# Attention on one core: six of the eight value products of the later queries split, masks side by side, and row maxima and the splits of w_o moved to earlier steps

## The chip, the cores and the metric

The kernel runs as one program on one core of a Trainium2 chip. The metric is the device time of one execution in microseconds (us); the time before is the median of three runs. A core has five engines that work side by side, each through its own queue in order: TensorE (PE in the profile, with its weight loads shown apart as PEld), VectorE (DVE), ScalarE (ACT), GpSimd (POOL) and SyncE (SP, which here only issues DMAs). PE reads SBUF and writes PSUM; DVE and ACT read and write both.

## The reference

Two layers of a decoder over 1024 positions. The change is in the attention of the first layer: 12 heads of dense causal attention (query and key of 96 columns, value of 64), in float32.

```python
def one_block(args):
    q_blk, n = args
    t_idx = n * Q_BLOCK + jnp.arange(Q_BLOCK)
    sc = jnp.einsum('bqhd,bkhd->bhqk', q_blk, k,
                    preferred_element_type=jnp.float32) * scale
    mask = k_idx[None, :] <= t_idx[:, None]
    sc = jnp.where(mask[None, None], sc, NEG)
    p = jax.nn.softmax(sc, axis=-1).astype(v.dtype)
    return jnp.einsum('bhqk,bkhd->bqhd', p, v)
```

Its result, with that of four more heads over a memory, goes through one output projection, `x = x + concat(mix, cross) @ w_o[i]`, and then through an MLP. The second layer has another attention, which the change does not touch.

## The kernel before

**Split products.** For most products of float32 accuracy a value is split in two parts, `hi` (rounded to the type float32r) and `lo` (the rest): `split` (lines 97 to 103) makes `hi` on ACT (line 99) and `lo` on DVE (line 100). A product is then three products of float32r: hi by hi, hi by lo, lo by hi. The alternative is one "whole" product in float32, which the profile shows as two records.

**One head.** For head h, `head_tiles` brings the 96 rows of query and key by four DMAs on SP's queue and splits them into qh, ql, kh, kl; there are three sets of these tiles, so it runs for head h + 2 while head h is computed. `row_max(h, i)` computes the scores of the 128 queries of tile i once, on PE, into the PSUM tile psx (two banks wide, one buffer, for tiles 4 to 7; a one-bank tile for 0 to 3), adds a causal mask with one bfloat16 product (identb by dmask, line 730), and lets DVE take the negative maximum of each row (line 731). After all eight tiles, `max_row` turns the maxima round on PE (psxt), splits them (mh, ml) and writes them by two DMAs on SP's queue as the 97th row of qh and ql, so that every later score has its row's maximum subtracted.

**Steps.** The scores are then computed again, transposed, in blocks: G is the half of the queries (0 earlier, 1 later, 512 columns each) and k the block of 128 keys. A block on the diagonal has fewer columns: for G = 1 the blocks 0 to 4 have 512, the blocks 5, 6 and 7 have 384, 256 and 128; for G = 0 the blocks 0 to 3 have 512, 384, 256 and 128. That makes NB = 12 blocks, or steps, a head, in the order of the table `blocks` (the last head has its own, `blocks_end`). Step n in program order is:

- `scores` (line 852): three products into a tile pss, with a mask product (identb by dmaskT) for a block on the diagonal; then ACT takes the exponential p (line 862), and p is split into ph and pl unless the block is "whole";
- the row maxima of a later head that the dictionary `ahead` assigns to step n;
- `values` (line 882) of the block of three steps ago (LV): for a whole block p by vf, for a split one ph by vh and ph by vl; and of the block of five steps ago (LB) the late third product, pl by vh. They add up in the tile pso, one for each G.

In steps with a narrow (128 column) block the score and value products are issued alternately. `v_tiles` (step 6 of a head) makes vh, vl and vf of the next head, with vf a full copy; a column of ones beside v gives the softmax's denominators. The finished pso goes through ACT (`on`, line 910) and two DMAs on SP; the denominators of heads 0 to 5, 6 to 9 and 10 are inverted in one go each (`rc_split`: DVE, ACT, and two DMAs rTq and rTk) and multiplied in by `rc_mul` (products psrc, lines 951 and 952, and a DVE multiplication). The last head is divided at once (`last_o`).

**What sets the order.** The recording layer keeps each engine's order close to that of the program, but may move a product behind a later one that does not wait for it. All DMAs of the stage are on SP's queue.

**w_o.** The first half of w_o is loaded and split during the last heads by `wq.step()`: eight actions (`load` or `split`, lines 628 and 99/100, tiles wor and woq, 128 by 1024 elements each), one every second step from step 120 (`n >= 10 * NB and n % 2 == 0`). The output projection (pswo, lines 108 to 110) follows the attention directly.

## Time and profile before

| | us |
|---|---|
| median of 3 runs | 2187.11 |
| lowest and highest of them | 2183.63, 2187.38 |
| the profiled execution, its own time | 2188.19 |
| its span, first to last instruction | 2186.5 |
| first score product of the attention stage starts (pss, line 852) | 253.40 |
| first product of w_o starts (pswo, line 108) | 488.30 |
| first product of the MLP's first layer starts (psu) | 584.55 |

The attention stage lies in the fifth to ninth of the 40 slices of the page's second part. How to read the profile: PE's records overlap, since a product begins before the one ahead of it has left the array, and their ends are modelled; the distance from start to start is what one costs. "x2" is the number of records that a row merges. Text in square brackets is the time that the engine was idle before the row and what ended it. In a view of stretches each row gives the limits, the length, and then for PE, PEld, DVE, ACT and POOL the busy time and the number of instructions, the clock of PE that was granted (1.00 is full), and the busy share of the DMA engines.

### The profile page before, as it was taken

The numbers are of one execution on the slowest core, as the hardware profiler recorded it, in microseconds if no ns is written. First come the engines' busy times: TensorE is split into PE (matmuls) and PEld (weight loads), VectorE is DVE, ScalarE is ACT, GpSimd is POOL, SyncE is SP. The second block draws the span as 40 slices with busy tenths as digits, with TensorE's granted clock in tenths as the row PEclk, the third lists the DMA queues.
The fourth block names the chain that finished last, engine by engine and source line by source line (L and its number), as shares of the span: only waits on it lengthen the run. The fifth ranks groups of instructions, "written<-read, shape, count | busy, mean of one in ns | idle before, by whom it ended". The sixth has DMA issues, their size and how long they took to land.

```text
span 2186.5 us, 28912 instructions
## 1 busy us (share of the span) xinstructions
PE 2139.8 (98%) x9993; PEld 1714.4 (78%) x9993; DVE 1480.1 (68%) x2813; ACT 1009.6 (46%) x2142; POOL 162.1 (7%) x227
## 2 busy tenths in 40 slices
PE   6999999999999999999999899999999999999998
PEld 5888776668788888888888778668788888888886
DVE  7556667755987776786657443665987776885665
ACT  5455466654633333444445453774633333444452
POOL 0012100001000000000001133440000000000000
PEclk9999999989999999999999999999999999999999
DMA  7202222323254445964533111123254445954442
GB/s 248 64 3 62 53 62 48 94 82 117 78 178 149 143 140 175 342 195 126 165 116 97 63 39 49 39 78 103 80 175 148 159 156 177 323 186 145 126 120 87
DMA packets 171232, 272.97 MB, mean 125 GB/s; under 512 B 15713, under 2 KB 71758, under 8 KB 171086
## 3 DMA queue, kind: packets, MB, share of 16 engines
q1 hardware_dynamic: 164228, 253.80, 36.6%
q0 software_dynamic: 4016, 13.12, 1.6%
q10 hardware_dynamic: 2842, 4.22, 0.5%
q8 instruction: 78, 1.28, 0.2%
q14 instruction: 68, 0.56, 0.1%
HBM read 181.69 MB, written 76.81 MB: 118 GB/s over the span
## 4 chain that ended last, share of the span: by engine, by line
PE 87%; DVE 6%; ACT 2%; DMA 2%; issue 1%; POOL 0%; SPq 0%; DVEq 0%; ACTq 0%; POOLq 0%
PE psy L1601 5%; PE psy L1603 5%; PE psy L1602 5%; PE psu L1316 5%; PE psu L1317 5%; PE psu L1315 5%; PE psz L1601 4%; PE psz L1602 4%; PE psz L1603 4%; PE pss L852 4%; PE psv L1317 4%; PE psv L1316 4%; PE psv L1315 4%; PE pso L882 4%; PE pswo L110 2%; PE pswo L108 2%
## 5 line engine op out<-in xcount | busy, mean ns | idle before, releaser
L99 ACT ACTIVATE i<-mr 128x512 fp32r<-128x512 f32 x78 | 49.3, 632 | 122.3 <-PE psu L1316 42.9
L862 ACT ACTIVATE p<-pss 128x512 f32<-128x512 f32 (+2 forms) x144 | 68.4, 486 | 80.3 <-PE pss L852 76.8
L1601 PE MATMUL psy<-g 128*128 128x512 f32 x256 | 99.9, 390 | 0.0
L1602 PE MATMUL psy<-g 128*128 128x512 f32 x256 | 99.6, 389 | 0.0
L1603 PE MATMUL psy<-g 128*128 128x512 f32 x256 | 99.4, 390 | 0.0
L99 ACT ACTIVATE g<-i 128x512 fp32r<-128x512 f32 x79 | 49.7, 629 | 92.0 <-PE psz L1602 45.1
L100 DVE TENSOR_TENSOR g<-i,g 128x512 fp32r<-128x512 f32 x79 | 55.2, 699 | 48.8 <-ACT g L99 48.8
L731 DVE TENSOR_REDUCE m<-psx 128x1 f32<-128x768 f32 (+7 forms) x96 | 71.3, 752 | 24.9 <-PE psx L730 24.4
L99 ACT ACTIVATE uh<-i 128x512 fp32r<-128x512 f32 x66 | 41.6, 631 | 85.3 <-PE psy L1602 40.7
L100 DVE TENSOR_TENSOR uh<-i,uh 128x512 fp32r<-128x512 f32 x66 | 45.5, 689 | 45.0 <-ACT uh L99 44.9
L1601 PE MATMUL psz<-g 128*128 128x512 f32 x192 | 74.7, 389 | 0.0
L1603 PE MATMUL psz<-g 128*128 128x512 f32 x192 | 74.7, 389 | 0.0
L1602 PE MATMUL psz<-g 128*128 128x512 f32 x192 | 74.7, 389 | 0.0
L100 DVE TENSOR_TENSOR i<-mr,i 128x512 fp32r<-128x512 f32 x78 | 53.6, 687 | 24.5 <-ACT i L99 24.5
L852 PE MATMUL pss<-qh,kh 97*128 97x512 f32 (+2 forms) x144 | 65.9, 464 | 0.5 <-DMA qh<-mhl 0.5
L882 PE MATMUL pso<-p,vf 128*128 128x512 f32 (+3 forms) x152 | 64.9, 509 | 0.0
L99 ACT ACTIVATE i<-d 128x512 fp32r<-128x512 f32 x44 | 27.8, 633 | 70.6 <-PE psu L1316 39.6
L852 PE MATMUL pss<-ql,kh 97*128 97x512 f32 (+2 forms) x144 | 58.4, 406 | 0.0
L1526 DVE TENSOR_TENSOR mqf<-mqq,mqf 128x512 f32<-128x512 f32 x64 | 43.0, 685 | 20.4 <-DMA mqq<-in_mlp_w_down_dram 20.1
L1603 PEld LDWEIGHTS psy<-g 128*128 128x128 f32 x256 | 48.0, 188 | 10.0
L1601 PEld LDWEIGHTS psy<-g 128*128 128x128 f32 x256 | 48.1, 188 | 9.9
L1602 PEld LDWEIGHTS psy<-g 128*128 128x128 f32 x256 | 48.1, 188 | 9.8
(623 smaller groups left out, 6901.6 us busy)
## 6 DMA issues: line engine op xcount, KB each, us to landing
i<-hd SPq DMA_DIRECT2D x154, 256.0 KB
hd<-uh SPq DMA_DIRECT2D x76, 256.0 KB
hd<-ul SPq DMA_DIRECT2D x76, 256.0 KB
mr<-in_mlp_w_up_dram SPq DMA_DIRECT2D x36, 512.0 KB
hd<-x SPq DMA_DIRECT2D x72, 256.0 KB
mr<-hd SPq DMA_DIRECT2D x70, 256.0 KB
d<-in_mlp_w_up_dram SPq DMA_DIRECT2D x32, 512.0 KB
mqq<-in_mlp_w_down_dram SPq DMA_DIRECT2D x32, 512.0 KB
```

Of the source, the lines that this page charges most:

```text
L99: nc.scalar.activation(hi, src, AF.Copy)
L100: nc.vector.tensor_tensor(lo, src, f32(hi), ALU.subtract)
L731: nc.vector.reduce_max(m8s[h][:, i : i + 1], ps[:, :n], axis=AX, negate=True)
L852: return lambda: nc.tensor.matmul(o, a, b, skip_group_check=True, **kw)
L862: nc.scalar.activation(p[:, c0:], ps, AF.Exp, scale=SC)
L882: mms.append(lambda: nc.tensor.matmul(o, a, b, skip_group_check=True, **kw))
L1315: nc.tensor.matmul(ps, wh[:, k, :], xh[:, k, :], start=p in (1, 2, 5) and k == 0, stop=False, skip_group_check=True)
L1316: nc.tensor.matmul(ps, wh[:, k, :], xl[:, k, :], start=False, stop=False, skip_group_check=True)
L1317: nc.tensor.matmul(ps, wl[:, k, :], xh[:, k, :], start=False, stop=k == 3, skip_group_check=True)
L1601: nc.tensor.matmul(ps, ah[:, j, :], bh, start=p in (1, 5, 2) and k == 0, stop=False, skip_group_check=True)
L1602: nc.tensor.matmul(ps, ah[:, j, :], bl, start=False, stop=False, skip_group_check=True)
L1603: nc.tensor.matmul(ps, al[:, j, :], bh, start=False, stop=k == NP - 1, skip_group_check=True)
```

## The change

- **Products.** For G = 1 only the blocks 0 and 2 stay whole; 4, 5, 6 and 7 are now split as 1 and 3 were. In the last head the four blocks of G = 0, whole before, are split too. There is one more buffer each for ph and pl.
- **vf** has one buffer for all heads instead of two; its copy is made two steps after vh and vl (`v_full`, step 8), and its ones are set once.
- **Order of blocks.** The two tables are new.
- **Masks of one step side by side.** In a step that is not interleaved and has a block on the diagonal, the row maximum's products are recorded between the first score product and the mask, so that the two masks follow one another. DVE's reduction is recorded after the split of the step.
- **Earlier steps.** The row maxima (`ahead`) stand one step sooner, but for the first pair, `head_tiles` two steps sooner (step 0), and the actions on w_o begin at step 116 instead of 120, one in three steps.

```diff
@@ row_max
-        nc.vector.reduce_max(m8s[h][:, i : i + 1], ps[:, :n], axis=AX, negate=True)
+        return lambda: nc.vector.reduce_max(m8s[h][:, i : i + 1], ps[:, :n], axis=AX, negate=True)
@@ v_tiles
-        vb = (at.tile([P, NT, 128], F32R, name=f"vh{i}"), at.tile([P, NT, 64], F32R, name=f"vl{i}"), at.tile([P, NT, 128], F32, name=f"vf{i}"))
+        vb = (at.tile([P, NT, 128], F32R, name=f"vh{i}"), at.tile([P, NT, 64], F32R, name=f"vl{i}"))
         vbufs.append(vb)
+    vf = at.tile([P, NT, 128], F32, name="vf")
+    nc.gpsimd.memset(vf[:, :, 64:128], 1.0)
...
-        nc.vector.tensor_copy(vf[:, :, 0:64], src)
-    blocks = [(1, 0), (0, 0), (1, 4), (0, 1), (1, 5), (0, 2), (1, 6), (0, 3), (1, 7), (1, 1), (1, 2), (1, 3)]
-    blocks_end = [(1, k) for k in (0, 1, 4, 3, 5, 2, 6, 7)] + [(0, k) for k in range(4)]
+    blocks = [(1, 0), (0, 0), (1, 4), (0, 1), (1, 2), (0, 2), (1, 5), (0, 3), (1, 1), (1, 6), (1, 7), (1, 3)]
+    WHOLE = {(1, 0), (1, 2)}
+    blocks_end = [(1, k) for k in (0, 4, 2, 5, 1, 6, 7, 3)] + [(0, k) for k in range(4)]
-    def whole(h, G, k):
-        return k not in (1, 3) if G else h == H - 1
@@ scores, then()
-            if whole(h, G, k):
-                probs[(h, G, k)] = (p,)
+            if (G, k) in WHOLE:
+                probs[(h, G, k)] = p
                 return
-            ph = at.tile([P, 512], F32R, tag="ph", bufs=3, name=f"ph{h}_{G}_{k}")
-            pl = at.tile([P, 512], F32R, tag="pl", bufs=4, name=f"pl{h}_{G}_{k}")
+            ph = at.tile([P, 512], F32R, tag="ph", bufs=4, name=f"ph{h}_{G}_{k}")
+            pl = at.tile([P, 512], F32R, tag="pl", bufs=5, name=f"pl{h}_{G}_{k}")
@@ values
+        if (G, k) in WHOLE:
+            if late:
+                return [], lambda: None
+            mm(po[:, c0:], vf[:, k, :], probs.pop((h, G, k))[:, c0:], start=first, stop=last)
+        elif late:
             mm(po[:, c0:], vh[:, k, :], probs.pop((h, G, k, "late"))[:, c0:], start=False, stop=last)
         else:
+            ph, probs[(h, G, k, "late")] = probs.pop((h, G, k))
+            mm(po[:, c0:], vh[:, k, :], ph[:, c0:], start=first, stop=False)
+            mm(po[0:64, c0:], vl[:, k, :], ph[:, c0:], start=False, stop=False)
+            last = False
@@ the loop over steps
+    def v_full(h):
+        nc.vector.tensor_copy(vf[:, :, 0:64], v[:, :, h * 64 : (h + 1) * 64])
...
-        for i, d in ((7, -4), (6, -2), (5, 0), (3, 1), (4, 2), (2, 3), (1, 5), (0, 6), (8, 7)) if h > 1 else ...
+        for i, d in ((7, -5), (6, -3), (5, -1), (4, 1), (3, 2), (2, 3), (1, 4), (0, 5), (8, 6)) if h > 1 else ...
...
-        for f in mix + ms:
+        rows_ = []
+        if mix or len(ms) < 4:
+            for f in mix + ms:
+                f()
+            ms = []
+        else:
+            ms.pop(0)()
+        for g, i in ahead.get(n, ()):
+            if i < NT:
+                rows_.append(row_max(g, i))
+            else:
+                max_row(g)
+        for f in ms:
             f()
         if n < len(seq):
             then_s()
-        for g, i in ahead.get(n, ()):
-            if i < NT:
-                row_max(g, i)
-            else:
-                max_row(g)
+        for f in rows_:
+            f()
...
             if h + 1 < H and j == 6:
                 v_tiles(h + 1)
-            if j == 2 and h + 2 < H:
+            if h + 1 < H and j == 8:
+                v_full(h + 1)
+            if j == 0 and h + 2 < H:
                 head_tiles(h + 2)
...
-        if n >= 10 * NB and n % 2 == 0:
+        if n >= 9 * NB + 8 and n % 3 == 0:
             wq.step()
```

How this moves instructions is shown at three places. **First, PE in the middle of head 4:** the numbers in a tile's name are the head, then G and k, or for psx the head and the query tile. Before, then with the change, the step of block (0, 2):

```order
L852 MATMUL pss4_0_2_3357<-qh1_2445,kh1_2447 128x256
L852 LDWEIGHTS identb_66
L852 MATMUL pss4_0_2_3357<-dmaskT_68,identb_66 128x128
L852 MATMUL pss4_0_2_3357<-ql1_2446,kh1_2447 128x256
L852 MATMUL pss4_0_2_3357<-qh1_2445,kl1_2448 128x256
L729 MATMUL psx5_1_3368<-kh2_2451,qh2_2449 128x256
L730 LDWEIGHTS identb_66
L730 MATMUL psx5_1_3368<-dmask_67,identb_66 128x128
L882 MATMUL pso4_1_3326<-p4_1_4_3305,vf0_2458 128x512
```

```order
L850 MATMUL pss4_0_2_3458<-qh1_2445,kh1_2447 128x256
L729 MATMUL psx5_0_3460<-kh2_2451,qh2_2449 128x128
L730 LDWEIGHTS identb_66
L730 MATMUL psx5_0_3460<-dmask_67,identb_66 128x128
L850 LDWEIGHTS identb_66
L850 MATMUL pss4_0_2_3458<-dmaskT_68,identb_66 128x128
L850 MATMUL pss4_0_2_3458<-ql1_2446,kh1_2447 128x256
L850 MATMUL pss4_0_2_3458<-qh1_2445,kl1_2448 128x256
L880 MATMUL pso4_1_3423<-ph4_1_4_3414,vh0_2456 128x512
L880 MATMUL pso4_1_3423<-ph4_1_4_3414,vl0_2457 64x512
```

The row maximum's products and its mask (line 730) now stand between the step's first score product and its mask, so the two products with identb are neighbours. The value products behind them are those of block (1, 4): one whole product before (p by vf), now two of three split ones (ph by vh and vl; pl by vh follows later).

**Second, DVE when w_o is split and the maxima of head 11 begin** (m8_11 from psx11_7, psx11_6, psx11_5; woq is a split of w_o). Before, then with the change:

```order
L100 TENSOR_TENSOR woq1_1_4695<-wor0_0_2_4601,woq1_1_4695 128x1024
L731 TENSOR_REDUCE m8_11_4438<-psx11_7_4439 128x1
L100 TENSOR_TENSOR pl9_1_1_4451<-p9_1_1_4448,ph9_1_1_4450 128x512
L731 TENSOR_REDUCE m8_11_4438<-psx11_6_4464 128x1
L100 TENSOR_TENSOR woq1_1_4695<-wor0_0_3_4665,woq1_1_4695 128x1024
L100 TENSOR_TENSOR pl9_1_3_4477<-p9_1_3_4474,ph9_1_3_4476 128x512
L731 TENSOR_REDUCE m8_11_4438<-psx11_5_4489 128x1
```

```order
L100 TENSOR_TENSOR woq1_1_5003<-wor0_0_2_4854,woq1_1_5003 128x1024
L100 TENSOR_TENSOR pl9_1_5_4629<-p9_1_5_4626,ph9_1_5_4628 128x384
L100 TENSOR_TENSOR pl9_0_3_4652<-p9_0_3_4649,ph9_0_3_4651 128x128
L731 TENSOR_REDUCE m8_11_4644<-psx11_7_4645 128x1
L100 TENSOR_TENSOR pl9_1_1_4663<-p9_1_1_4660,ph9_1_1_4662 128x512
L954 COPY vf_2460<-v_1436 128x8x64
L100 TENSOR_TENSOR pl9_1_6_4682<-p9_1_6_4679,ph9_1_6_4681 128x256
L731 TENSOR_REDUCE m8_11_4644<-psx11_6_4672 128x1
L100 TENSOR_TENSOR pl9_1_7_4701<-p9_1_7_4698,ph9_1_7_4700 128x128
L731 TENSOR_REDUCE m8_11_4644<-psx11_5_4708 128x1
L100 TENSOR_TENSOR woq1_1_5003<-wor0_0_3_4952,woq1_1_5003 128x1024
L100 TENSOR_TENSOR pl9_1_3_4715<-p9_1_3_4712,ph9_1_3_4714 128x512
```

Before, the third split of w_o stands directly ahead of the maximum of tile 7, and the fourth and one subtraction ahead of that of tile 5. With the change two subtractions lie between the third and tile 7, and the fourth stands behind tile 5, ahead of tile 4. The new splits pl9_1_5, pl9_1_6 and pl9_1_7 and the copy vf are between them.

**Third, the start of head 11:** first SP's queue, with the two DMAs of head 11's maxima (to qh2 and ql2) and the two of the inverted denominators of heads 6 to 9 (rTq and rTk), before and with the change.

```order
L911 DMA fa1_87<-on9_1_4561 64x512
L914 DMA den6_2463<-on9_1_4561 4x1x128
L939 DMA rTq321_4609<-rch1_4605 4x8x128
L939 DMA rTk321_4610<-rcl1_4606 4x8x128
L718 DMA qh2_2449<-mh11_4627 1x8x128
L719 DMA ql2_2450<-ml11_4628 1x8x128
```

```order
L907 DMA fa1_87<-on9_1_4809 64x512
L910 DMA den6_2463<-on9_1_4809 4x1x128
L718 DMA qh2_2449<-mh11_4834 1x8x128
L719 DMA ql2_2450<-ml11_4835 1x8x128
L935 DMA rTq321_4862<-rch1_4858 4x8x128
L935 DMA rTk321_4863<-rcl1_4859 4x8x128
```

The maxima's DMAs have moved ahead of rTq and rTk. On PE the first products of head 11, before and with the change:

```order
L882 MATMUL pso10_1_4534<-pl10_1_3_4675,vh0_2456 128x512
L852 MATMUL pss11_1_0_4678<-qh2_2449,kh2_2451 128x512
L951 MATMUL psrc1_0_512_4691<-rTq321_4609,sel_2465 128x512
L952 MATMUL psrc1_0_512_4691<-rTk321_4610,sel_2465 128x512
L852 MATMUL pss11_1_1_4698<-qh2_2449,kh2_2451 128x512
L951 MATMUL psrc1_1_512_4709<-rTq321_4609,sel_2465 128x512
L952 MATMUL psrc1_1_512_4709<-rTk321_4610,sel_2465 128x512
L852 MATMUL pss11_1_4_4713<-qh2_2449,kh2_2451 128x512
L852 MATMUL pss11_1_0_4678<-ql2_2450,kh2_2451 128x512
```

```order
L880 MATMUL pso10_1_4775<-ph10_1_1_4885,vl0_2457 64x512
L850 MATMUL pss11_1_0_4935<-qh2_2449,kh2_2451 128x512
L880 MATMUL pso10_0_4796<-pl10_0_3_4876,vh0_2456 128x128
L850 MATMUL pss11_1_0_4935<-ql2_2450,kh2_2451 128x512
L880 MATMUL pso10_1_4775<-ph10_1_6_4900,vh0_2456 128x256
L850 MATMUL pss11_1_0_4935<-qh2_2449,kl2_2452 128x512
L880 MATMUL pso10_1_4775<-ph10_1_6_4900,vl0_2457 64x256
L947 MATMUL psrc1_0_512_4948<-rTq321_4862,sel_2465 128x512
L948 MATMUL psrc1_0_512_4948<-rTk321_4863,sel_2465 128x512
```

Before, head 10's value products are all ahead of head 11's first score; behind it come first score products (qh by kh) of three blocks and reciprocal products, and the first product that reads ql2 is the ninth row. With the change the product that reads ql2 is the fourth row, two behind head 11's first score product, and head 10's value products lie between the scores.

21 lines of the change are left out of this document (5 added, 16 removed).

## The prediction

> **What bounds the kernel now.** I read the page first (its busy times and the chain of work that ended last), then the table of busy time and granted clock over stretches of the attention stage, then the timeline of single engines there. The page has a span of 2186.5 us (the profiled execution took 2188.19 us, 1.1 us above the median of 2187.11):
>
> ```profile
> span 2186.5 us, 28912 instructions
> ...
> PE 2139.8 (98%) x9993; PEld 1714.4 (78%) x9993; DVE 1480.1 (68%) x2813; ACT 1009.6 (46%) x2142; POOL 162.1 (7%) x227
> ...
> PE 87%; DVE 6%; ACT 2%; DMA 2%; issue 1%; POOL 0%; SPq 0%; DVEq 0%; ACTq 0%; POOLq 0%
> ```
>
> TensorE (PE) is busy 98% of the span and makes 87% of the chain that ended last. Other stages are not touched, so the question is how long PE needs for the attention stage, whose start and end stand in the table above. Each row below is one stretch: its limits, its length, then busy time and instructions of PE, weight loads (PEld), VectorE (DVE), ScalarE (ACT) and GpSimd, the granted PE clock, the DMA share.
>
> ```profile
> 310.00:330.00 20.00, 20.00 (x106) 13.74 (x105) 14.30 (x23) 13.93 (x28) 0.00 (x0) 1.00 0.29 64
> 376.00:410.00 34.00, 33.53 (x156) 21.28 (x155) 21.92 (x33) 18.23 (x36) 0.00 (x0) 1.00 0.24 61
> 437.20:440.64 3.44, 1.92 (x11) 1.28 (x10) 3.20 (x4) 2.44 (x4) 0.00 (x0) 0.99 0.39 112
> 440.64:444.05 3.41, 3.41 (x10) 2.44 (x8) 2.38 (x3) 1.64 (x3) 0.00 (x0) 0.51 0.26 82
> 459.60:464.53 4.93, 4.90 (x15) 2.17 (x14) 1.58 (x3) 2.03 (x4) 0.00 (x0) 0.99 0.20 46
> 464.53:478.18 13.65, 13.65 (x29) 7.43 (x27) 4.20 (x7) 4.82 (x9) 0.00 (x0) 0.50 0.15 50
> ```
>
> The first row is the stage when all goes well: PE busy 20.00 of 20.00 us at clock 1.00, DVE 14.30 (72%), ACT 13.93 (70%). There a microsecond less of PE work is a microsecond less of time. A head has 95 PE records by the code (36 score products, 12 of row maxima, 16 masks, 18 of split and 12 of whole products, a turn), so at 106 in 20.00 us it takes 17.9 us, a step 1.5. The last four rows are two accidents. In 437.20 to 440.64 PE is busy for only 1.92 of 3.44 us, and the 3.41 us that follow run at half clock. In 459.60 to 464.53 PE starts only 15 products in 4.93 us, and then 13.65 us run at clock 0.50. Half clock costs half its length: 3.41 x 0.49 = 1.7 us and 13.65 x 0.50 = 6.8 us.
>
> **Products: six of eight key blocks split, where two were.** In the timeline of PE the end of a record is modelled, so I price a product by the distance to the next start. Columns: start, duration, line, operation, tiles, count. A whole f32 product (p,vf) appears as two records, a split one as three (pl,vh; ph,vh; ph,vl).
>
> ```profile
> 301.42 0.23 PE L852 MATMUL pss<-qh,kh 97*128 97x128 f32 x1
> 301.49 0.86 PE L882 MATMUL pso<-p,vf 128*128 128x384 f32 x2
> 302.18 0.22 PE L852 MATMUL pss<-dmaskT,identb 128*128 128x128 bf16 x1
> ...
> 304.70 0.60 PE L882 MATMUL pso<-p,vf 128*128 128x256 f32 x2
> 304.94 0.58 PE L852 MATMUL pss<-qh,kh 97*128 97x512 f32 x1
> 305.36 0.28 PE L882 MATMUL pso<-pl,vh 128*128 128x256 f32 x1
> 305.48 0.40 PE L852 MATMUL pss<-ql,kh 97*128 97x512 f32 x1
> ...
> 306.94 0.38 PE L882 MATMUL pso<-p,vf 128*128 128x128 f32 x2
> 307.08 0.48 PE L852 MATMUL pss<-ql,kh 97*128 97x512 f32 x1
> 307.40 0.39 PE L852 MATMUL pss<-qh,kl 97*128 97x512 f32 x1
> ...
> 309.61 1.02 PE L882 MATMUL pso<-p,vf 128*128 128x512 f32 x2
> 310.47 0.22 PE L852 MATMUL pss<-dmaskT,identb 128*128 128x128 bf16 x1
> ...
> 312.60 0.48 PE L882 MATMUL pso<-pl,vh 128*128 128x512 f32 x1
> 312.91 0.39 PE L882 MATMUL pso<-ph,vh 128*128 128x512 f32 x1
> 313.37 0.33 PE L852 MATMUL pss<-qh,kh 97*128 97x384 f32 x1
> 313.55 0.23 PE L852 MATMUL pss<-dmaskT,identb 128*128 128x128 bf16 x1
> 313.59 0.42 PE L852 MATMUL pss<-ql,kh 97*128 97x384 f32 x1
> 313.85 0.34 PE L852 MATMUL pss<-qh,kl 97*128 97x384 f32 x1
> ```
>
> 512 columns: whole 309.61 to 310.47 = 0.86; split, 3 x 0.23 (two of them from 312.91 to 313.37) = 0.69. 384 columns: whole 301.49 to 302.18 = 0.69; split 3 x 0.18 (313.37 to 313.55) = 0.54. 256: whole plus one 512 score product is 304.70 to 305.36 = 0.66, less 0.23 = 0.43; split 3 x 0.12 (305.36 to 305.48) = 0.36. 128: 306.94 to 307.40 = 0.46, less 0.23 = 0.23; split 3 x 0.07 (301.42 to 301.49) = 0.21. Gain of one set of four widths: 0.17 + 0.15 + 0.07 + 0.02 = 0.41 us. There are 13 sets: blocks 4 to 7 of the later queries in 12 heads, and the four blocks of the earlier queries in the last head, which were whole. **-5.3 us.** Bounds: -6.1 (10 ns less for each split product of 384 and 128 columns, the rounding of these rows) and +2.1 (second rival).
>
> Each split adds one ACT conversion and one DVE subtraction:
>
> ```profile
> L100 DVE TENSOR_TENSOR pl<-p,ph 128x512 fp32r<-128x512 f32 x27 | 18.4, 683 | 7.2 <-ACT ph L99 7.2
> ...
> L100 DVE TENSOR_TENSOR pl<-p,ph 128x128 fp32r<-128x128 f32 x10 | 2.8, 284 | 0.7 <-ACT ph L99 0.7
> ```
>
> DVE takes 683 ns at 512 columns and 284 ns at 128, so about 550 and 417 between: 1.93 us a head; I put ACT at the same. In a head of 17.9 us DVE goes from 72% to about 82%, ACT from 70% to about 80%. They work beside PE; if that cover went, the full 1.93 us a head would show. DVE feeds PE through the row maxima: their single large PSUM tile (psx) is free only when DVE has reduced it. I charge **+1.0 us** for small waits (bounds 0 and the third rival).
>
> **Masks side by side.** A mask product costs 0.04 us (313.55 to 313.59) and slows the product after it: 313.59 to 313.85 is 0.26 where a 384 product alone takes 0.18, so 0.08 more and 0.12 us in all. The change puts two masks next to each other twice a head for heads 1 to 11: 22 pairs. No pair stands in the trace; between nothing saved and the whole delay of one mask (22 x 0.08 = 1.8) I take the middle: **-1.0 us.**
>
> **The first accident.**
>
> ```profile
> 436.91 1.23 DVE L100 TENSOR_TENSOR woq<-wor,woq 128x1024 fp32r<-128x1024 f32 x1 [1.77 <-ACT woq L99]
> 438.05 1.22 DVE L731 TENSOR_REDUCE m<-psx 128x1 f32<-128x1024 f32 x1
> ...
> 439.32 0.67 PE L729 MATMUL psx<-kh,qh 96*128 96x512 f32 x2 [1.52 <-DVE m L731]
> ```
>
> PE's next row maximum (psx, 439.32) waited 1.52 us on DVE's reduction at 438.05, which stood behind a w_o split (woq, 436.91, 1.23 us) that itself waited for ACT. In the changed order two narrow subtractions (384 and 128 columns) lie between that split and this maximum, and the four w_o splits are three steps apart instead of two and start four steps sooner. So this wait should go: **-1.5 us**, and its half clock: **-1.7 us.** What is late next: the same splits now stand beside denser DVE work, one of them between maxima 5 and 4 of head 11; that is part of the next charge.
>
> **The second accident.**
>
> ```profile
> 455.19 0.27 PE L711 MATMUL psxt<-ident,m 128*8 128x128 f32 x1
> ...
> 464.62 0.63 PE L852 MATMUL pss<-ql,kh 97*128 97x512 f32 x1
> ...
> 456.76 0.25 ACT L99 ACTIVATE mh<-psxt 8x128 fp32r<-8x128 f32 x1
> ...
> 456.68 0.67 SPq L939 DMA_DIRECT2D rTq<-rch  x1
> ...
> 458.95 0.64 SPq L719 DMA_DIRECT2D ql<-ml  x1
> ```
>
> The maxima of head 11 are turned round on PE at 455.19 (psxt), but ACT converts them only at 456.76, behind the reciprocal's conversion, and on SP's queue their two DMAs stand behind rTq (456.68) and its partner. The second (ql) is issued at 458.95 and the products that read it start at 464.62. Until then PE can issue only the first of head 11's score products and reciprocal products (psrc). In the change the last maximum comes one step sooner, and both DMAs stand ahead of rTq. The new block order also lets head 10's products run between head 11's scores. The 15 records of 459.60 to 464.53 are worth one whole product (0.86) and 13 x 0.23 = 3.0 us, so about **-1.1 us** of waiting goes, and with it the long half clock: **-6.8 us.** Bounds of this whole edit: 0 (the clock falls anyway) and -7.9.
>
> The Trainium skill, "TensorE: Matmul & The Clock Gate", section "Part 1: The HAM clock gate", says that the clock follows a free-running activity window of about 3.4 us, falls after an idle one and returns after one busy one. The lengths agree with the rows (3.41, and 13.65 is four times that). The return does not: PE is recorded busy 13.65 of 13.65 us in the last row of the table of stretches, and the clock stayed low. By the page a new wait would cost 1.7 us of clock; by that row it can cost 6.8.
>
> **What the change costs elsewhere.** At the start two heads' preparation meets the first maxima:
>
> ```profile
> 250.00:270.00 20.00, 19.30 (x102) 13.03 (x100) 16.96 (x24) 13.20 (x25) 1.92 (x4) 1.00 0.29 68
> ```
>
> DVE is at 16.96 of 20.00 us there, its fullest stretch of the stage. The change adds 1.93 us a head and draws head 2's tiles two steps and its maxima one step forward. Bounds: 0 (the 3.04 us left over hold it) and 3.9 (all of two heads' new splits); nearest to full, I take **+2.0 us.** At the end the last four blocks now need exp, ph, pl and a late product where a whole one followed exp: two more hand-offs of about 0.3 us (the 284 ns row) and two more steps, with nothing left to interleave; **+1.0 us** (0 to 2.5). A new wait of this kind may drop the clock once for 3.4 us: **+1.7 us** (0 to 6.8). The full-block copy vf has one buffer instead of two; its copy comes at step 8, after the last product that reads it (step 7), so I cost it at nothing; the first head's two fills by GpSimd become one, off PE's path.
>
> **Sum.** -5.3 + 1.0 - 1.0 - 1.5 - 1.7 - 1.1 - 6.8 + 2.0 + 1.0 + 1.7 = -11.7 us. 2188.2 - 11.7 = 2176.5 for an execution like the profiled one; 1.1 lower for the median: **2175.4 us.** After the attention PE goes straight into w_o, so what is won there should arrive at the end.
>
> **Rivals.** *The clock falls anyway (20%).* The 13.65 us at half clock may come from the reciprocal products (psrc), which stay, or move to the crowded start or end. For: they stand in the stretch before it. Against: six pairs of them, for heads 0 to 5, lie in the stretch 376 to 410, at clock 1.00, where two pairs stand ahead of the slow stretch. The 6.8 us stay instead of the 1.7 charged, with 1.1 of waits: 2175.4 + 6.2 = 2181.6 us.
>
> *Split products are no cheaper (8%).* Every product has its own weight load, of 188 ns:
>
> ```profile
> L1603 PEld LDWEIGHTS psy<-g 128*128 128x128 f32 x256 | 48.0, 188 | 10.0
> ```
>
> If each had to wait for it, a split would cost at least 3 x 0.188 = 0.56: at 128 columns 0.33 more than a whole, at 256 0.13 more, at 384 0.13 less, at 512 0.17 less as before. That is +0.16 a set, +2.1 in all instead of -5.3: 2182.8 us. The 0.06 to 0.07 us between 128-wide products above speak against it.
>
> *DVE becomes the bound (8%, slower).* With one psx tile, a reduction that stands behind one more subtraction stops PE as at 439.32. One such stop of 1.5 us in each of heads 1 to 10, half of them followed by 3.4 us at half clock: 15 + 5 x 1.7 = 23.5: 2198.9 us. It decides once DVE's work in a step is longer than PE's step of 1.5 us, as where a 1.22 us reduction (438.05), a 1.23 us split (436.91) and a new subtraction meet. For: DVE at 82%. Against: at 72% PE's own wait for it is a single one in the whole stage (total, times, longest):
>
> ```profile
> PE psx L729 <- DVE m L731: 1.5, 1, 1.5
> ```
>
> *More is won (14%).* The start and the end hide their costs and no clock falls: 2175.4 - 2.0 - 1.0 - 1.7 - 1.0 = 2169.7 us.
>
> That leaves 50% for the forecast, with its own range of 2172 to 2179.
>
> **Range and chances.** From the better case to past the clock rival: 2168 to 2185 us. Measurement tells apart about 0.2% (4.4 us), so faster is below 2182.7, slower above 2191.5. Faster: 50 + 14 + about 14 of the 28 of the first two rivals = 78%. The rest of those, 14%, within 0.2%. Slower: 8%.
>
> **What would show it.** The groups of p,vf have 48 records of 512 columns and no narrower ones; pl and ph of 384, 256 and 128 columns about double; a head in the middle of the stage takes about 17.4 us instead of 17.9; clock 1.00 where the last two heads run; ql of head 11 landed before its first score; w_o begins about 12 us sooner. I am wrong if PE waits on DVE's maxima show in several heads, if a row of the stage at clock 0.5 is longer than 3.4 us, or if the middle heads do not get shorter.

## The result and the profile after

The changed kernel is not faster: median 2185.98 us of 20 executions against 2183.99 us of 20 before, ratio 1.0015 with a 95% interval of 1.0002 to 1.0028. A second set of 12 executions, in the experiments below, gave 2187.13 us and the same ratio and interval. 2175.4 us was forecast; the first median lies one microsecond above the upper end of the range, 2185.

The two profiled executions alone say the opposite: 2182.75 us after, 2188.19 before. The page after, its span, busy times and chain:

```profile
span 2181.0 us, 29215 instructions
...
PE 2130.9 (98%) x10045; PEld 1715.8 (79%) x10045; DVE 1503.2 (69%) x2865; ACT 1034.2 (47%) x2194; POOL 161.6 (7%) x226
...
PE 89%; DVE 4%; ACT 2%; DMA 2%; issue 1%; POOL 0%; DVEq 0%; SPq 0%; ACTq 0%; POOLq 0%
```

The granted clock explains the contradiction. Call the span times (1 - mean granted clock) the clock loss of an execution. Before, the profiled execution had a mean clock of 0.991, a loss of 19.7 us, where 133 executions average 14.02; after, it had 0.995, a loss of 10.9, where 32 executions average 18.65. (The clock is recorded to three digits, which is 2.2 us in a single execution and little in such means.) One pair of profiles cannot be subtracted here. On average the time rose by 2.86 us (2186.90 against 2184.04 us): the clock loss by 4.63, and all other work fell by 1.77.

The stretches after that answer to those of before, in the same columns:

```profile
250.00:270.00 20.00, 18.52 (x100) 13.29 (x98) 17.34 (x26) 14.40 (x29) 1.52 (x3) 1.00 0.34 80
310.00:330.00 20.00, 20.00 (x114) 14.55 (x111) 16.46 (x26) 16.12 (x33) 0.00 (x0) 1.00 0.24 58
425.00:445.00 20.00, 19.65 (x112) 14.36 (x111) 18.50 (x29) 16.99 (x34) 0.00 (x0) 1.00 0.43 128
460.00:478.00 18.00, 18.00 (x87) 11.92 (x87) 11.36 (x16) 12.43 (x29) 0.00 (x0) 1.00 0.23 67
577.12:583.95 6.83, 5.76 (x14) 4.51 (x15) 6.78 (x14) 3.15 (x6) 0.00 (x0) 0.50 0.03 12
```

In the middle DVE and ACT went from 72% and 70% to 82% and 81%, as forecast, and PE stays full. The last heads (third and fourth row) run at clock 1.00, also as forecast. But PE is idle 1.5 us in the first row, and the last row is a new half-clock stretch, outside the attention. w_o's first product (pswo) starts at 477.41 us instead of 488.30, 10.9 us sooner. What happened to those 10.9 us stands 100 us later, in the timeline of PE and of ACT:

```profile
477.41 0.39 PE L108 MATMUL pswo<-woq,x 128*128 128x512 f32 x1
...
573.61 1.29 PE L1179 MATMUL psT_m<-ident,d 128*128 128x128 f32 x8
578.19 0.79 PE L1327 MATMUL psu<-mqq,uh 128*128 128x512 f32 x1 [3.29 <-ACT x L1182]
```
```profile
576.47 0.59 ACT L1182 ACTIVATE x<-psT_m 128x512 f32<-128x512 f32 x1
576.94 0.63 ACT L99 ACTIVATE g<-x 128x512 fp32r<-128x512 f32 x1
577.54 0.60 ACT L1182 ACTIVATE x<-psT_m 128x512 f32<-128x512 f32 x1
```

The first product of the next stage (psu) waits 3.29 us until ACT has copied the last transposed tile (psT_m) out of PSUM. Before, the same instructions ran in the same order without this wait:

```profile
583.24 1.29 PE L1167 MATMUL psT_m<-ident,d 128*128 128x128 f32 x8
584.55 0.49 PE L1315 MATMUL psu<-mqq,uh 128*128 128x512 f32 x1
```

What I take to be different is the PSUM banks that the pool hands out. The numbers below are those of the compiled programs; no view of the profile shows them, and the runs e1_bank and e4_bankin put them to the test:

```
tile                         before   changed
psT_m, block 3, halves 0, 1  4, 5     4, 1
psu 0 (two banks)            0-1      0-1
```

The tile that is read last has landed in a bank that psu needs. Why it lands there is argued, not shown: the attention frees its PSUM tiles in another order now, so the rotation of six banks would stand at another place 100 us later.

In heads 0 and 1, behind the first score product, PE waits five times, 2.71 us in all, where before it waited once, 0.57 us, on ACT's ph:

```profile
268.34 0.56 PE L729 MATMUL psx<-kh,qh 96*128 96x512 f32 x2 [0.50 <-DVE m L731]
270.01 0.68 PE L729 MATMUL psx<-kh,qh 96*128 96x512 f32 x2 [0.46 <-DVE m L731]
271.95 0.61 PE L729 MATMUL psx<-kh,qh 96*128 96x512 f32 x2 [0.20 <-DVE m L731]
273.69 0.56 PE L729 MATMUL psx<-kh,qh 96*128 96x512 f32 x2 [1.05 <-DVE m L731]
275.42 0.50 PE L880 MATMUL pso<-pl,vh 128*128 128x512 f32 x1 [0.50 <-DVE pl L100]
```

The lengths of heads are taken from first score product to first score product; for heads 2 and 6, before, and for heads 0, 2 and 6, after, these are:

```profile
289.67 0.40 PE L852 MATMUL pss<-qh,kh 97*128 97x512 f32 x1
...
361.49 0.39 PE L852 MATMUL pss<-qh,kh 97*128 97x512 f32 x1
```
```profile
252.12 0.73 PE L850 MATMUL pss<-qh,kh 97*128 97x512 f32 x2 [0.54 <-DMA qh<-mhl]
...
291.46 0.39 PE L850 MATMUL pss<-qh,kh 97*128 97x512 f32 x1
...
362.30 0.40 PE L850 MATMUL pss<-qh,kh 97*128 97x512 f32 x1
```

Heads 0 and 1 take 289.67 - 253.40 = 36.27 us before and 291.46 - 252.12 = 39.34 after; a middle head (361.49 - 289.67) / 4 = 17.95 before and 17.71 after.

### The profile page after: what moved, and what is told of

It is laid out like the page before. It is cut to its first block, busy times and chain, and to the rows that moved or that the text cites. A ratio compares the mean times of both kernels' runs of the same rounds, so it can differ in the third digit from the quotient of the medians.

```text
span 2181.0 us, 29215 instructions
## 1 busy us (share of the span) xinstructions
PE 2130.9 (98%) x10045; PEld 1715.8 (79%) x10045; DVE 1503.2 (69%) x2865; ACT 1034.2 (47%) x2194; POOL 161.6 (7%) x226
## 4 chain that ended last, share of the span: by engine, by line
PE 89%; DVE 4%; ACT 2%; DMA 2%; issue 1%; POOL 0%; DVEq 0%; SPq 0%; ACTq 0%; POOLq 0%
PE psu L1328 5%; PE psu L1329 5%; PE psu L1327 5%; PE psy L1613 5%; PE psy L1615 5%; PE psy L1614 5%; PE psz L1614 4%; PE psz L1615 4%; PE psz L1613 4%; PE psv L1327 4%; PE psv L1329 4%; PE psv L1328 4%; PE pss L850 4%; PE pso L880 3%; PE pswo L110 3%; PE pswo L108 3%
## 5 line engine op out<-in xcount | busy, mean ns | idle before, releaser
L860 ACT ACTIVATE p<-pss 128x384 f32<-128x384 f32 (+3 forms) x144 | 69.0, 485 | 46.0 <-PE pss L850 43.0
L731 DVE TENSOR_REDUCE m<-psx 128x1 f32<-128x1024 f32 (+7 forms) x96 | 71.7, 752 | 15.5 <-PE psx L730 15.2
L100 DVE TENSOR_TENSOR pl<-p,ph 128x512 fp32r<-128x512 f32 (+3 forms) x120 | 62.0, 525 | 25.2 <-ACT ph L99 23.8
L850 PE MATMUL pss<-ql,kh 97*128 97x384 f32 (+3 forms) x144 | 62.3, 432 | 0.0
L99 ACT ACTIVATE ph<-p 128x512 fp32r<-128x512 f32 (+3 forms) x120 | 59.6, 502 | 2.9
```

The source lines that it names most:

```text
L99: nc.scalar.activation(hi, src, AF.Copy)
L100: nc.vector.tensor_tensor(lo, src, f32(hi), ALU.subtract)
L731: return lambda: nc.vector.reduce_max(m8s[h][:, i : i + 1], ps[:, :n], axis=AX, negate=True)
L850: return lambda: nc.tensor.matmul(o, a, b, skip_group_check=True, **kw)
L860: nc.scalar.activation(p[:, c0:], ps, AF.Exp, scale=SC)
```

## The experiments

All times at full clock below are worked out in the same way: from such starts, less half of each stretch at half clock. "w_o" is the time from its first product to psu. Median, ratio and clock loss (a mean) are over all executions of a run, the other columns are those of its one profiled execution. Each ratio is to the kernel before, run beside it.

| run | median us (n) | ratio, 95% interval | clock loss | heads 0+1 | middle head | attention | w_o |
|---|---|---|---|---|---|---|---|
| before | 2184.4 (133) | | 14.0 | 36.27 | 17.95 | 226.4 | 96.3 |
| changed | 2186.0 (20) | 1.0015, 1.0002 to 1.0028 | 18.8 | 39.34 | 17.71 | 225.3 | 100.3 |
| a0_after | 2187.1 (12) | 1.0015, 1.0002 to 1.0028 | 18.4 | 39.34 | 17.71 | 225.4 | 100.1 |
| e0_before | 2184.1 (12) | 0.9989, 0.9974 to 1.0005 | 14.0 | 36.28 | 17.95 | 226.9 | 96.2 |
| e1_bank | 2181.0 (12) | 0.9986, 0.9970 to 1.0002 | 13.3 | 39.33 | 17.71 | 225.3 | 97.5 |
| e4_bankin | 2187.3 (12) | 1.0011, 1.0000 to 1.0023 | 16.9 | 36.26 | 17.95 | 226.6 | 99.0 |
| e2_whole | 2180.5 (12) | 0.9976, 0.9962 to 0.9990 | 11.3 | 38.64 | 17.82 | 225.6 | 97.8 |
| e3_timing | 2184.6 (12) | 1.0001, 0.9984 to 1.0018 | 17.7 | 37.03 | 17.72 | 222.2 | 97.8 |
| e5_start | 2181.4 (12) | 0.9994, 0.9979 to 1.0010 | 14.7 | 37.87 | 17.73 | 224.0 | 97.4 |
| e9_tiles | 2180.5 (12) | 0.9992, 0.9982 to 1.0003 | 11.8 | 38.19 | 17.73 | 224.3 | 97.5 |
| e6_end | 2179.4 (12) | 0.9981, 0.9967 to 0.9995 | 12.7 | 37.46 | 17.72 | 223.2 | 96.6 |
| e7_spread | 2178.1 (12) | 0.9977, 0.9965 to 0.9990 | 12.7 | 37.64 | 17.73 | 223.4 | 96.5 |
| e8_wholeend | 2176.9 (12) | 0.9971, 0.9961 to 0.9981 | 9.1 | 37.05 | 17.83 | 224.0 | 96.7 |
| e10_both | 2175.9 (7) | 0.9966, 0.9951 to 0.9980 | 8.4 | 36.49 | 17.82 | 223.3 | 96.7 |
| x1_padbefore | 2176.9 (10) | 0.9971, 0.9961 to 0.9981 | 10.9 | 36.27 | 17.95 | 222.8 | 96.8 |
| x3_ql11 | 2178.8 (11) | 0.9981, 0.9969 to 0.9993 | 9.9 | 36.30 | 17.95 | 225.8 | 96.3 |
| x2_padspread | 2172.1 (6) | 0.9947, 0.9931 to 0.9963 | 10.1 | 37.28 | 17.72 | 218.8 | 97.1 |
| x4_all | 2171.0 (6) | 0.9940, 0.9923 to 0.9957 | 9.4 | 36.49 | 17.82 | 218.9 | 97.3 |

### Both kernels once more: e0_before, a0_after

> The kernel before, unchanged, for a second profiled execution. Theory (the half clock is a matter of the single execution): the stretch of 13.65 us at half clock in the last heads, which the prediction booked as a gain of 6.8 us, is shorter or missing here, or the stretches lie in other stages, while the order and the waits are the same; ratio 1.000 within 0.002. Rival (the late ql forces it): the same stretch of about 13 us at half clock stands behind the wait at about 460 us again.

> The changed kernel, unchanged, for a second profiled execution and more times. Theory (its waits are fixed, the half clock they bring is not): the idle time before the first psu is 3.3 us again, heads 0 and 1 take 39.3 us again; half-clock stretches stand behind one or both of these places, longer than the 6.83 us of the first profile where the mean clock is under 0.993; median near 2186 us. Rival (the first measurement was disturbed by chance): median at most 2182 us.

The rival held for the kernel before, and my theory for its ratio: the stretch of 13.65 us stands in the same place again. It is tied to its place, but not there in every execution, or 133 of them would not average 14.0 us of loss where this one has 17.5. (It stands in e4_bankin's profile too, at 460.37 us.)

```profile
463.20:476.85 13.65, 13.65 (x31) 7.35 (x30) 3.71 (x6) 4.82 (x9) 0.00 (x0) 0.50 0.21 71
```

The changed kernel came out as forecast: 3.3 us in front of psu, 39.34 us, 2187.13 us. Only the profile was again one at 0.995, so where its worse executions lose their clock is inferred from the next runs, not seen.

### The bank: e1_bank, e4_bankin

e1_bank is the changed kernel with one tile in another bank; e4_bankin does the reverse to the kernel before: two other tiles (one of pswo, one of psT_m) go into the banks of psx, so that the last psT_m lands in bank 0.

```diff
-                ps = ps1(f"psT_m{layer}_{t}_{i}")
+                ps = psx("psT3")[:, 0:512] if (layer, t, i) == (0, 3, 1) else ps1(f"psT_m{layer}_{t}_{i}")
```

> The changed kernel with one transposed tile (psT of the fourth query block, second half) written into the two PSUM banks of the tag x instead of a bank of the tag m; nothing else differs. Theory (banks): the changed allocation order leaves that tile in one of the two banks that the first psu product needs, so PE must wait for its last reader; then the idle time of 3.29 us before the first psu falls below 0.7 us, the half clock behind it goes too in most executions, and the time falls by 3.3 to 5 us against the changed kernel, to about 2181 to 2183 us. Rival (ACT is late there because w_o now begins sooner): the idle time stays above 2.5 us and the time stays at about 2186 us.

> The kernel before with nothing changed but the PSUM banks of two tiles at the end of the w_o stage, chosen so that the fourth block's second transposed tile stands in bank 0, which the first psu product needs; no instruction is added or moved in the attention. Theory (banks): PE idles 2.5 to 3.5 us before the first psu as in the changed kernel, and the time rises by 3 us for the wait and by up to 5 us more where the clock halves behind it: median 2187 to 2192 us. Rival (the wait in the changed kernel came from its earlier start of w_o): idle time under 0.7 us, median near 2184 us.

PE's rows there, first e1_bank, then e4_bankin:

```profile
573.66 0.66 PE L1179 MATMUL psT<-ident,d 128*128 128x128 f32 x4
574.40 0.50 PE L1327 MATMUL psu<-mqq,uh 128*128 128x512 f32 x1
575.46 0.50 PE L1328 MATMUL psu<-mqq,uh 128*128 128x512 f32 x1 [0.55 <-DVE mqq L100]
```
```profile
579.89 0.66 PE L1167 MATMUL psT_m<-ident,d 128*128 128x128 f32 x4
583.84 0.80 PE L1315 MATMUL psu<-mqq,uh 128*128 128x512 f32 x1 [3.29 <-ACT x L1170]
```

The wait goes with the bank and comes with the bank; an earlier w_o has no part in it. Without it the changed kernel gains 5.1 us on average (2186.9 to 2181.9, 95% within 2.4), and the clock loss falls by 5.4. With it the kernel before is 2.6 us slower (2184.0 to 2186.7, within 2.0), and the clock loss rises by 2.9. So nearly all the price is clock: most of the 3.29 us themselves come back, since behind the wait PE no longer stops for mqq and mqf, as it does in e1_bank (the row at 575.46, and 0.64 us 13 us later).

### Products against timing: e2_whole, e3_timing

e2_whole puts back the whole products with their buffers. e3_timing puts back the moments of maxima, tiles and w_o splits, and with them the recording of the masks: no two masks are neighbours in it.

```diff
+    def whole(h, G, k):
+        return k not in (1, 3) if G else h == H - 1
...
-            if (G, k) in WHOLE:
+            if whole(h, G, k):
```
```diff
-        for i, d in ((7, -5), (6, -3), (5, -1), (4, 1), (3, 2), (2, 3), (1, 4), (0, 5), (8, 6)) if h > 1 else ...
+        for i, d in ((7, -4), (6, -2), (5, 0), (3, 1), (4, 2), (2, 3), (1, 5), (0, 6), (8, 7)) if h > 1 else ...
...
-        for f in ms:
+        for f in mix + ms:
             f()
...
-            if j == 0 and h + 2 < H:
+            if j == 2 and h + 2 < H:
...
-        if n >= 9 * NB + 8 and n % 3 == 0:
+        if n >= 10 * NB and n % 2 == 0:
```

> The changed kernel with the whole and split products of before (blocks 0, 2, 4 to 7 whole for the later queries; ph and pl with 3 and 4 buffers, vf with two), the rest as changed. Theory (the split crowds DVE at the start, and is worth less than priced in the middle): heads 0 and 1 together go back from 39.3 to about 36.5 us, a middle head takes 17.85 to 17.95 us against 17.69 changed and 17.95 before, the three last heads keep their gain (about 56 us against 58.5 before). Rival 1 (the moved maxima and tiles are what costs at the start): heads 0 and 1 stay at 38.5 us or more. Rival 2 (the masks side by side bring the whole gain of the middle heads and the split none): a middle head takes 17.7 us. If the banks theory holds, PE waits less than 0.7 us before the first psu, since here that tile lands in another bank.

> The changed kernel with the moments of before for the row maxima, the head tiles and w_o's splits; the products and the order of blocks as changed. Theory (splits crowd the start): heads 0 and 1 still take 38 us or more, a middle head 17.7 us, and the three last heads go back to about 58.5 us at full clock. Rival 1 (moved maxima and tiles cost at the start): heads 0 and 1 take about 36.5 us. Rival 2 (the gain of the last heads comes from the block order and the split): the three last heads take 56 us. PE waits less than 0.7 us before the first psu by the banks theory, as the tile lands elsewhere here as well.

Whole products cost a middle head only 17.82 - 17.71 = 0.11 us, and the kernel is not slower for them: e2_whole has no wait in front of psu, so it is compared with e1_bank, 2180.5 against 2181.0 us. e3_timing's middle head takes 17.72 us, as in the changed kernel, so moved moments and neighbouring masks together are worth nothing there. At the start my theory missed: without the splits heads 0 and 1 still take 38.64, with the old moments 37.03. So 2.3 of the 3.1 us come from the moved moments, the other 0.8 from the splits and the new order. The theory on the last heads missed too: with the old moments heads 9 to 11 take 55.2 us at full clock, no more than changed (55.6). What the moments bring there is clock alone: e3_timing has 10.2 us at half clock at 463 us again, and as much behind a wait at the start:

```profile
268.80:272.20 3.40, 2.15 (x11) 1.26 (x9) 2.94 (x5) 2.32 (x4) 0.00 (x0) 1.00 0.03 7
272.20:282.40 10.20, 10.20 (x29) 6.65 (x28) 5.40 (x8) 4.56 (x8) 0.00 (x0) 0.50 0.35 78
```

PE was idle for 1.25 us of 3.40, and the next 10.20 us run at half clock.

### Start and end: e5_start, e9_tiles, e6_end, e7_spread

On top of the mended bank (in these four with one or two tiles of pswo in the banks of psx besides): e5_start has head 2's maxima and the tiles of heads 2 and 3 at the old steps. e9_tiles has only the tiles of heads 2 and 3 there; its expectation speaks of all heads, but the edit moves these two. e7_spread (second piece of the diff) has maxima and tiles up to two steps later still, and e6_end (third piece) is e5_start with the last head's end eased, as e7_spread is too.

```diff
-        for i, d in ((7, -5), (6, -3), (5, -1), (4, 1), (3, 2), (2, 3), (1, 4), (0, 5), (8, 6)) if h > 1 else ...
+        for i, d in ((7, -5), (6, -3), (5, -1), (4, 1), (3, 2), (2, 3), (1, 4), (0, 5), (8, 6)) if h > 2 else ((7, -4), (6, -2), (5, 0), (3, 1), (4, 2), (2, 3), (1, 5), (0, 6), (8, 7)) if h > 1 else ...
...
-            if j == 0 and h + 2 < H:
+            if j == (2 if h < 2 else 0) and h + 2 < H:
```
```diff
+        for i, d in ... if h > 2 else ((7, -2), (6, 0), (5, 2), (3, 3), (4, 4), (2, 5), (1, 6), (0, 7), (8, 8)) if h > 1 else ...
...
+            if j == (4 if h < 2 else 0) and h + 2 < H:
```
```diff
-    blocks_end = [(1, k) for k in (0, 4, 2, 5, 1, 6, 7, 3)] + [(0, k) for k in range(4)]
+    blocks_end = [(1, k) for k in (0, 4, 3, 5, 1, 6, 7, 2)] + [(0, k) for k in range(4)]
...
+    def whole(h, G, k):
+        return (G, k) in WHOLE or (h == H - 1 and G == 0)
...
-            if (G, k) in WHOLE:
+            if whole(h, G, k):
```

> The changed kernel with the bank mended and with head 2's row maxima and the tiles of heads 2 and 3 made at the steps of before; later heads as changed. Theory (it is the moved maxima and tiles that meet head 1's at the start): heads 0 and 1 together take 37.0 us as with the timing of before, against 39.3 changed; the half clock that follows the waits there goes in most executions; median 2177 to 2180 us. Rival (the splits make the waits, wherever the maxima stand): heads 0 and 1 take over 38.3 us and the median stays at 2181 us.

> The changed kernel with the bank mended and only the tiles of all heads made two steps later again, as before; the row maxima of every head as changed. It tells the two moved things apart. Theory (the maxima of head 2 beside head 1's are what waits at the start): heads 0 and 1 still take 38.8 us or more. Rival (the tiles' subtractions of 1.2 us each are what waits): heads 0 and 1 take 37.9 us or less, as with both put back (37.87).

> The kernel of the run before this one with the last head's end eased too: its blocks for the earlier queries whole again, and block 2, a whole product, as the last block of its later queries, so that the long reciprocal starts earlier and no subtraction stands behind it. Theory: the waits of PE in the first 4 us of w_o (0.3 and 0.4 us in the changed kernel) go, and the time is 0.5 to 1.5 us shorter than in the run before this one: 2176 to 2179 us, the best of the study. Rival (those waits are hidden by others behind them): no difference above 0.5 us.

> The kernel e6_end with head 2's row maxima two steps later than in the kernel before and the tiles of heads 2 and 3 two steps later, so that they stand apart from head 1's. Theory (the waits of 0.24 and 1.18 us at about 267 and 271 us come from head 2's maxima right behind head 1's, and their half clock of 10.24 us too): both waits go, heads 0 and 1 take 36.5 us against 37.46 in e6_end, no half-clock stretch stands at 272 us in the profile, and the time is 1 to 4 us shorter: 2176 to 2178.5 us. Rival (the splits alone overfill VectorE at the start, the work only shifts): heads 0 and 1 take 37.3 us or more and the time does not move.

e5_start brings 1.5 us of the 2.3, not all, and neither its time nor its clock loss (14.7 against 13.3 us) is better than e1_bank's; e9_tiles lies between both of its cases and decides nothing. In e6_end PE's two waits at the start of w_o are gone, as expected, and w_o takes 96.6 instead of 97.4 us; its median is 1.9 us lower, more than the 0.5 to 1.5 expected, but the executions scatter too much to tell that from nothing. In e7_spread the rival was right about the work: heads 0 and 1 take 37.64, and the wait has only changed its name.

```profile
271.20 0.78 PE L883 MATMUL pso<-ph,vh 128*128 128x512 f32 x1 [1.12 <-ACT ph L99]
```

Its time fell by 1.3 us at the median, which these intervals do not tell from nothing.

### The split alone: e8_wholeend, e10_both

e8_wholeend goes with e6_end, e10_both with e7_spread; the kernels of a pair differ by the whole products and their buffers, and in e8_wholeend by the bank of one tile of pswo.

> The kernel e6_end with the whole and split products of before (blocks 0, 2, 4 to 7 of the later queries whole), so that it differs from e6_end by the split alone, with the banks, the start and the end mended in both. Theory (the split is worth 0.11 us a head in the middle and gives it back at the start): attention stage at full clock within 0.8 us of e6_end's 223.2 us, time within 2 us of 2179.4 us. Rival (the prediction's price of 0.41 us a head): 4 to 5 us longer than e6_end, about 2184 us.

> The kernel e7_spread with the whole and split products of before: the lightest VectorE of all. Theory (what the change was worth lies in the order, not in the split): heads 0 and 1 take about 36 us, a middle head 17.82 us, clock losses the least of the study, time 2176 to 2178.5 us, not slower than e7_spread. Rival (the split carries the gain): 3 us or more slower than e7_spread.

The attention takes 224.0 against 223.2 us, and 223.3 against 223.4: the split saves nothing, or 0.8 us. The times are 2.6 us (95% within 2.8) and 2.4 us (within 2.2) lower on average without it, the clock losses 3.6 and 4.3 us lower; in e8_wholeend that is lower than either case had it. What the change was worth lay in its order, not in its products: e8_wholeend, without the new splits, takes 0.9971 of the kernel before.

### Why the clock falls in the last heads: x1_padbefore, x3_ql11, x2_padspread, x4_all

e6_end and e7_spread showed half clock behind a stretch in which PE waits for nothing; these are e6_end's rows:

```profile
459.40:462.80 3.40, 3.40 (x15) 1.75 (x14) 1.55 (x3) 1.76 (x5) 0.00 (x0) 1.00 0.19 44
462.80:469.60 6.80, 6.80 (x16) 3.55 (x16) 2.45 (x4) 1.74 (x4) 0.00 (x0) 0.50 0.00 0
```

The reciprocal products stand in it, of 1 to 6 rows. The padding gives them 128:

```diff
-    sel = at.tile([6, 6, 64], F32R, name="sel")
+    sel = at.tile([P, 6, 64], F32R, name="sel")
+    nc.gpsimd.memset(f32(sel), 0.0)
...
-                w = sel[0:n, 2 * j : 2 * j + m, :].rearrange("p h c -> p (h c)")
+                w = sel[:, 2 * j : 2 * j + m, :].rearrange("p h c -> p (h c)")
...
-        rT = [hb.tile([6, S], F32R, tag=e, bufs=1, name=f"rT{e}{c}")[: n // NT] for e in ("q32", "k32")]
+        rT = [hb.tile([P, S], F32R, tag=e, bufs=1, name=f"rT{e}{c}") for e in ("q32", "k32")]
...
+            nc.gpsimd.memset(f32(rT[e]), 1.0)
```

> The kernel before with the reciprocal products (psrc) contracted over 128 rows instead of 1 to 6: the rows added to sel are zero, those added to the reciprocals are one, so that the results are the same; two fills by GpSimd come before each group. Theory (few rows make TensorE look idle to its clock): the stretch of 13.65 us at half clock at about 463 us is gone or at most 3.4 us, the mean loss by the clock falls from about 14 to 10 us, the time to about 2180 us. Rival (the late ql alone): the 13.65 us stand there again.

> The kernel before with head 11's row maxima and tiles at the moments of the changed kernel and nothing else changed. Theory of the prediction (late ql): ql of head 11 lands before its first scores, PE does not run thin at 460 us, and the long half-clock stretch at 463 us goes (at most 3.4 us): mean loss by the clock about 10 us, time about 2180 us. Rival (reciprocal products): a stretch of 6.8 us or more stands there still, time about 2183 us.

> The kernel e7_spread with the same padding of the reciprocal products. Theory (few rows): no half clock between 440 and 480 us, mean loss by the clock falls from 12.7 to about 9.5 us, time to about 2175 us. Rival (it is chance or the split products): loss and time as in e7_spread, within 1.5 us.

> The kernel e10_both (changed order, whole products of before, head 2's maxima and the tiles of heads 2 and 3 two steps later, bank and end mended) with the padding of the reciprocal products. Theory (the split is worth nothing, the padding 4 us of work and some clock): about 2170.5 us, within 1.5 us of x2_padspread's 2172.1 or below it, no half clock between 250 and 480 us. Rival (the split pays once the clock is steady): 2 us or more above x2_padspread.

In the kernel before, each of the two remedies takes the stretch away. In x1_padbefore ql of head 11 is as late as before (its DMA is issued at 455.59 us, the scores start at 458.81), yet the stretch is gone:

```profile
461.00:474.65 13.65, 13.65 (x65) 9.29 (x64) 5.40 (x8) 6.99 (x15) 1.84 (x2) 1.00 0.39 123
```

In x3_ql11 the thin products stay and ql is early (issued at 451.99 us, scores from 456.19), and the stretch is gone as well. One profile each would prove little, but the executions agree: 9 of the 10 of x1_padbefore and 10 of the 11 of x3_ql11 have a mean clock of 0.995 or more, against 49 of 133 before. So in this kernel it took late data and thin products together.

That is no rule for the others. In e6_end and e7_spread ql is early too (issued at 453.18 and 449.49 us, scores from 458.59 and 454.91), and 6.8 us of half clock stand there all the same; the two profiles of the changed kernel and that of e10_both, with thin products and early ql, have none. What tells these apart stays open. x2_padspread, which pads e7_spread, has none at this place, as its theory said; its clock loss fell from 12.7 to 10.1 us, and 10.24 us of half clock at 271.82 us stayed.

The padding also shortens work: the attention takes 222.8 instead of 226.4 us, and 218.8 instead of 223.4 in x2_padspread, with seven fills more on GpSimd, six of 0.95 us and one of 0.43. The rows of the reciprocal products, in e0_before and padded, one after the other:

```profile
485.52 0.44 PE L951 MATMUL psrc<-rTq,sel 1*64 1x512 f32 x1
485.81 0.38 PE L952 MATMUL psrc<-rTk,sel 1*64 1x512 f32 x1
486.12 0.49 PE L882 MATMUL pso<-p,vf 128*128 128x128 f32 x2
```
```profile
459.04 0.40 PE L953 MATMUL psrc<-rTq,sel 128*128 128x512 f32 x1
459.28 0.39 PE L954 MATMUL psrc<-rTk,sel 128*128 128x512 f32 x1
459.51 0.40 PE L852 MATMUL pss<-qh,kh 97*128 97x512 f32 x1
```

From start to start these are 0.29 and 0.31 us with one row, 0.24 and 0.23 with 128. Over all pairs, the second product takes 0.32 us on average before (at full clock) and 0.23 padded; the first takes 0.33 and 0.38, longer in a few places. So most of the gain stands around them: head 7, with twelve of these products, takes 23.4 us before and 21.1 padded, of which its score products give 0.7 us, its whole value products 1.0 and the reciprocal products 0.3. Why their neighbours gain is not shown. x4_all, the changed order without the split, with bank, start and end mended and the products padded, is the best: 2171.0 us, 0.9940 (0.9923 to 0.9957) of the kernel before. x2_padspread, with the split, took 2172.1; the pair is not told apart.

## Why the prediction was wrong, point by point

**Products, -5.3 us: mis-sized.** The split was worth 0 to 1 us of work. The whole products were priced rightly; the split ones were priced by the shortest distances in the timeline, 1.80 us for a set of twelve products (0.69 + 0.54 + 0.36 + 0.21). Over heads 2 to 5, the distances from each product to the next start are, per head and in us:

```
                             e2_whole     changed
value products, whole        3.08         1.03
value products, split        3.46         5.46
score products               8.30         8.10
row maxima, masks, turns     2.99         3.12
sum                         17.83        17.71
```

The whole set cost 2.05 and 0.20 more on the scores beside it, 2.25 in all, near the 2.21 of the prediction. The split set costs 2.00 and 0.13 more on the maxima and masks. Averages of the split products in the profile before would have said 1.96. The rival on the split (no cheaper) came near in its result, not by its mechanism: in the changed kernel's middle heads a split product of 128 columns takes 0.09 us on average, less than the 0.188 us of a weight load.

**Small waits, +1.0 us: large enough.** From 300 us to the end of the attention PE waits on DVE's maxima twice, 0.6 us together, and on ACT twice, again 0.6 us together.

**Masks side by side, -1.0 us: not borne out as a sum.** A pair stands in these rows of the changed kernel:

```profile
330.13 0.23 PE L730 MATMUL psx<-dmask,identb 128*128 128x128 bf16 x1
330.20 0.22 PE L850 MATMUL pss<-dmaskT,identb 128*128 128x128 bf16 x1
330.23 0.48 PE L850 MATMUL pss<-ql,kh 97*128 97x512 f32 x1
330.55 0.39 PE L850 MATMUL pss<-qh,kl 97*128 97x512 f32 x1
```

The pair takes 0.10 us and the product behind it 0.32 instead of 0.23, 0.19 in all, where two single masks at the prediction's 0.12 us make 0.24. By these rows a pair saves what was booked. But e3_timing, without any pair, has the same middle head: the pairs and the moved maxima together gain nothing there, and the two were not run apart. If the parts add up, the 0.13 us between the kernel before (17.95) and e2_whole (17.82) come from the new order of blocks, which the sum put at nothing in the middle heads.

**First accident, -1.5 and -1.7: right in the place, not in the reason.** The wait of 1.52 us is down to 0.35 in the row below; no half clock stands there. The distance between w_o's splits was not needed for it: x3_ql11 leaves them where they were, moves only the maxima and tiles of head 11, and has no wait there; e3_timing, with the old moments of both and the new order of blocks, has none either.

```profile
437.13 0.67 PE L729 MATMUL psx<-kh,qh 96*128 96x512 f32 x2 [0.35 <-DVE m L731]
```

**Second accident, -1.1 and -6.8: right in its mechanism, too large in its clock, and half the cause.** ql is issued at 450.73 us now and head 11's scores start at 456.15; no half clock followed in either profile. But 6.8 us was what one execution lost. x3_ql11 takes both accidents, booked at 11.1 us, out of the kernel before, and gains 4.4 us on average (2184.0 to 2179.6, 95% within 1.8): it loses 4.1 us less by the clock, where 8.5 were booked, and its attention takes 0.6 us less at full clock (226.4 to 225.8), where 2.6 were. And the rival on the reciprocal products had half the cause: padding them also ends the stretch.

**Start, +2.0: too small.** It was 3.07 us (39.34 - 36.27), from the moved moments more than from the new splits.

**End, +1.0: right.** PE's waits when w_o starts and what goes with them make 97.5 - 96.3 = 1.2 us in e1_bank; easing the end (e6_end against e5_start) takes 0.8 us off w_o and 0.3 off the last three heads.

**One new half-clock stretch, +1.7: far too small.** The changed kernel loses 18.65 us by the clock on average, the least of the study is 8.4 (e10_both). Of these 10 us 5.4 go with the bank. Where the rest falls was not seen, since both profiles of the changed kernel have no half clock in the attention; waits at the start bring such stretches in e3_timing and e5_start.

**"After the attention PE goes straight into w_o, so what is won there should arrive at the end": wrong, and not in the sum at all.** 10.9 us arrived at w_o; in front of psu 3.29 us and, with it, the clock were given back, by a PSUM bank.

In sum: -4.9 us of work and -6.8 of clock were booked; -1.8 and +4.6 were measured. At full clock heads 0 and 1 take 3.1 us more, heads 2 to 8 1.3 less and heads 9 to 11 2.9 less; w_o takes 4.0 more, most of which comes back behind it. If the parts add up, the 11.4 us that the clock is off are 4.4 for taking the half clock of one execution for the kernel's (8.5 booked, 4.1 in x3_ql11), 5.4 for the wait in front of psu, which the sum did not have, and 1.6 for the rest. That wait alone turned the sign: without it (e1_bank) the mean is 2.2 us below the kernel before, which its interval, 0.9970 to 1.0002, does not quite tell from nothing.

Of the signs named for being wrong, the first came: waits on the maxima (2.8 us, 6 times), four of them in heads 0 and 1 and one each in heads 8 and 9. The second came only outside the stage: its rows stay at clock 1.00, and the row of 6.83 us at clock 0.5 stands in front of and behind psu. The third did not come, but the middle heads got shorter by 0.24 us instead of 0.5.

```profile
PE psx L729 <- DVE m L731: 2.8, 6, 1.1
```

## What to carry to other kernels

Take a kernel's clock loss from many executions, and price its half-clock stretches by that mean; a gain that is mostly clock can be lost again wherever the change opens a gap of a microsecond. After a change in the order of a stage, look at the buffers the pool hands out in the stages behind it: a tile in another bank can make the first product of the next stage wait for the last reader of this one. Price a group of products by the mean distance over a whole stretch, never by the shortest one.
